# How the expert weights of a two-layer MoE backbone are laid over the partitions when they are loaded

## The chip, the cores and the metric

The kernel runs on one core of one Trainium2 chip. The metric is the device time of one execution in microseconds (us), given as the median of several runs. The kernel before takes 1938.27 us, the median of three runs (1936.55 to 1939.51).

## The reference

The reference is a trunk of two layers over 512 latent tokens and 256 context tokens of width 1024. Layer 0 is attention beside a gated MLP, layer 1 is a bidirectional state-space scan (S5). Each is followed by a mixture of experts, in which every token chooses two of 32 experts, and a last RMSNorm ends it. Cut to what matters here:

```
x = x + m_lat[2] * y_lat                        # mixer of the layer
f = modulate(x, norm_ffn_g, ...)                # (T, 1024); T = 768 in layer 0, 512 in layer 1
top 1 of 4 groups, top 2 of its 8 experts -> two experts and two weights per token
expert e:  (silu(xblk @ w1[e]) * (xblk @ w3[e])) @ w2[e]
           w1[e], w3[e]: (1024, 512)    w2[e]: (512, 1024)    all float32
x = x + m_lat[5] * (sum over a token's two experts of weight * expert(token))
```

The order in which the 1024 features of a token are summed in `xblk @ w1[e]` is free, as long as the features of the tokens and the rows of the matrix are taken in the same order.

## The kernel before

Each layer has a mixer stage and then an expert stage (`moe`, line 1165). In the expert stage `ffn_in` (L884) makes the normalized and modulated features with the features on the partitions (`fT`), multiplies them by the router, and writes the tokens to a DRAM scratch `fD`, one row of 1024 floats per token. For that its inner function `rows` (L918) turns 8 blocks of 128 features by 128 tokens with TensorE into a PSUM tile of 128x1024, copies this to SBUF with ScalarE (L924), and issues the write of 512 KB from ScalarE's queue (L925). There are 6 such tiles in layer 0 and 4 in layer 1. `route` (L944) then makes the tables of which token goes to which expert, on VectorE with small matmuls.

The loop over the 32 experts (L1281) does the following for one expert. GpSimd gathers the expert's tokens from `fD` by an indirect DMA (`gather`, L1088), issued two experts ahead. TensorE turns them (`gathered_T`, L1096) so that the features lie on the partitions in 8 blocks of 128, numbered k. `expert_block` (L1106) then multiplies by W1 and W3, summing over k in PSUM (L1123), forms silu(.) * (.) on ScalarE and VectorE, turns the result (L1135), multiplies by W2 (L1145), weighs it (L1153), and GpSimd scatters it to a DRAM scratch `yD` (L1161). A first block holds 64 tokens; where an expert has more, every engine branches into further blocks (`overflow`, L1254 to L1265). Expert 31 is computed in `finish` (L1328), which also adds both contributions of each token to the residual.

In layer 0 the loop has side work between the experts: `s5_ahead` prepares the S5 parameters of layer 1 on TensorE, VectorE, ScalarE and GpSimd, with small DMAs of its own. One of its results is the DRAM scratch `wD` (L1494), of shape (128, 16, 2, 2, 128). Later, in the mixer of layer 1, `W[i]` is loaded from it in two DMAs (L1859), in each of which partition p takes the block `wD[p, 8*i:8*i+8]`, 8 x 2 x 2 x 128 floats that lie together.

The weights of an expert are three loads of 2048 KB, W1, W3 and W2, issued by SP through `Chunks.load` (L165), `wload` (L211) and `fetch` (L221). `fetch` lets a load start only when the load two before it has landed (`AHEAD = 2`), so that two are in flight. The tiles come from a ring of buffers for some three experts; a load also waits until its buffer was read by the last matmul that used it. Each expert's block ends with `ch.load(3)`, which puts three further loads into SP's order.

The layout of a load is set in L172: `"(k p) n -> p k n"` with p = 128. For W1 and W3, of shape (1024, 512), partition p takes the rows p, 128 + p, ..., 896 + p: 8 rows of 2 KB that lie 256 KB apart. For W2, of shape (512, 1024), it takes 4 rows of 4 KB. Block k of the gathered features meets `Wx[:, k]` in L1123, so feature k * 128 + p of a token meets row k * 128 + p of the matrix.

Of the kernel before, what the change touches and what calls it, by code (L numbers as in the profile page):

```python
# [20 lines left out]
KD = 8  # L21
# [73 lines left out]
class HiLo:  # L95
# [7 lines left out]
    def load(self, m=1):  # L103

        k = self.k
        for _ in range(m):
            r = self.stage.tile([128, self.per, self.n], F32, name="wraw", tag="wraw", bufs=NST2 if self.runs else NST)
            k.fetch(r, self.src[:, self.loaded:self.loaded + self.per])
            self.raw.append(r)
            self.loaded += self.per  # L110
# [48 lines left out]
class Chunks:  # L159
# [5 lines left out]
    def load(self, n=1):  # L165
        k, l = self.k, self.l
        for _ in range(n):
            i = len(self.w)
            if i == 96:
                return  # L170
            e, c = divmod(i, 3)
            src = (k.in_moe_w1, k.in_moe_w3, k.in_moe_w2)[c][l, e].rearrange("(k p) n -> p k n", p=128)  # L172
            pool = self.ring.pop(0)
            self.w.append(k.wload(src, (KD, 512) if c < 2 else (4, 1024), pool=pool))
            if pool is not self.once:
                self.ring.append(pool)


class Kernel:
# [704 lines left out]
    def ffn_in(self, l, tiles, pool, fD, lg):  # L884

        nc = self.nc
        nt = len(tiles)
        t0 = tiles[0]
        wr, br = self.wr, self.br
        A = self.scale1(l, 4, self.gffn[l], f"Affn{l}")  # L890
        S = self.M[l][:, 3]
        fT = pool.tile([128, KD, nt * 128], F32, name="fT")

        spare = [self.X[:, t] for t in range(t0)]
        nf = 5 - t0
        groups = [[(0, NCT, NT - NCT)] + ([(1, 0, NCT)] if t0 == 0 else [])]
        lT = pool.tile([128, 256], F32, name="lT", tag="lT", bufs=1)
        nc.gpsimd.memset(lT, 0.0)
        for tiles_ in self.features(fT, A, S, groups, t0, pool, nf, spare=spare):

            i0, hn = tiles_[0] - t0, len(tiles_) // 2
            q = self.pa([128, hn * 128], name="pl")
            for k in range(KD):
                for h in range(2):
                    at = (i0 + h * hn) * 128
                    nc.tensor.matmul(q[64 * h:64 * h + 36], wr[:, k], fT[:, k, at:at + hn * 128], start=(k == 0),
                                     stop=(k == KD - 1), tile_position=(0, 64 * h))
            for h in range(2):
                hs = slice(64 * h, 64 * h + 36)
                self.evac(lT[hs, :hn * 128], q[hs])  # L910
            p = self.pa([128, hn, 128], name="plT")
            for i in range(hn):
                nc.tensor.transpose(p[:, i], lT[:, i * 128:(i + 1) * 128], self.ident)
            for h in range(2):
                nc.vector.tensor_add(lg[:, i0 + h * hn:i0 + (h + 1) * hn], p[:, :, 64 * h:64 * h + 36],
                                     br[:, None, :].to_broadcast([128, hn, 36]))

        def rows(i):  # L918
            p = self.pb("pfr")
            f = pool.tile([128, D], F32, name="f", tag="fxh", bufs=nf)  # L920
            for k in range(KD):
                self.mark_rows = nc.tensor.transpose(p[:, k // 4, (k % 4) * 128:(k % 4 + 1) * 128],
                                                     fT[:, k, i * 128:(i + 1) * 128], self.ident)
            nc.scalar.copy(f.rearrange("p (a n) -> p a n", a=2), p)  # L924
            nc.scalar.dma_start(fD[i * 128:(i + 1) * 128], f)  # L925

        for i in range(nt):
            rows(i)
# [557 lines left out]
    def s5_ahead(self):  # L1486
# [13 lines left out]
        with ExitStack() as es:  # L1500
# [95 lines left out]
            with tc.tile_pool(name="s5v", bufs=1) as tp:  # L1596
# [43 lines left out]
                def kernel(g2):  # L1640
# [4 lines left out]
                    nc.scalar.copy(kv, p[:, g2 % 2])  # L1645

                load(0)
                yield
                for g2 in range(16):
                    load(g2 + 1)  # L1650
                    s, l = divmod(g2, 2)
                    xs = slice(4 * s + l, 4 * s + 4, 2)
                    br, bi = raw.pop(g2)
                    Q = [x[:, xs, None].to_broadcast([128, 2, 16]) for x in (qr, qi)]
                    b0 = tp.tile([128, 2, 16], F32, name="b0", tag="b0")
                    b1 = tp.tile([128, 2, 16], F32, name="b1", tag="b1")
                    tm = tp.tile([128, 2, 16], F32, name="bt", tag="bt5")
                    self.after(v.tensor_mul(b0, br, Q[0]), self.mark_dve)
                    v.tensor_mul(tm, bi, Q[1])
                    v.tensor_sub(b0, b0, tm)  # L1660
                    v.tensor_mul(b1, br, Q[1])
                    v.tensor_mul(tm, bi, Q[0])
                    v.tensor_add(b1, b1, tm)
                    tm = self.pb("pE")[:, 0, 0:256].rearrange("p (d i q) -> p d i q", d=2, i=8)
                    E[g2] = self.cpair(v, tp, [x[:, xs] for x in le], (b0, b1), 2, "E", 1, tm)
                    yield
                    if g2:
                        kernel(g2 - 1)
                    products(g2)
                    yield  # L1670
# [407 lines left out]
```

## Time and profile before

| what | value |
|---|---|
| median of three runs | 1938.27 us (1936.55 to 1939.51) |
| the profiled execution's own time | 1946.14 us |
| its span (first to last instruction) | 1944.5 us |
| mean granted TensorE clock | 0.918 of full speed |
| read from DRAM, written to DRAM | 513.41 MB, 32.60 MB |
| loads of expert weights | 192 of 2048 KB, on SP's queue |
| expert stage of layer 0, first matmul of expert 0 to that of expert 31 | 450.7 to 1098.5 us |
| expert stage of layer 1, first matmul of expert 0 to that of expert 31 | 1368.6 to 1903.8 us |

All times of the profile belong to one execution, and are counted from the span's start. PE is TensorE, PEld its weight loads, DVE VectorE, ACT ScalarE, POOL GpSimd, SP SyncE; a q behind an engine's name is its sequencer. L1123 is line 1123 of the kernel. Matmuls are pipelined and their ends are modelled, so that TensorE's busy time is no measure of how near it is to its peak. A wait for several semaphores is put down to the one that came last by the profile. Queue q1 holds the DMAs that SP issues, q10 those of ScalarE, q0 GpSimd's; q8 and q14 fetch instructions.

### The profile page before, as it was taken

To read this page: it belongs to the slowest core of one execution; us is meant where nothing else is said; L and a number is where in the kernel's file an instruction comes from. 1 tells how busy PE (TensorE), PEld (TensorE's weight loads), DVE (VectorE), ACT (ScalarE), POOL (GpSimd) and SP (SyncE) were. 2 spreads that over 40 slices of the span, in tenths; PEclk is the share of its full clock that TensorE was granted. 3 is DMA by queue.
4 is the path that set the end of the run, shared out by engine and by line. 5 is a ranking of instruction groups with operands and counts; after the bars stand their busy time and mean duration, and the time that the engine had idled before them with its cause. 6 is when DMAs were issued, how large, how long until landed. Compare 5 with 4: busy or idle time off the path is not lost. (4 is left out here: it accounts for less than half of the span.)

```text
span 1944.5 us, 30168 instructions
## 1 busy us (share of the span) xinstructions
PE 1534.8 (79%) x11383; PEld 976.6 (50%) x11383; DVE 699.3 (36%) x1842; ACT 325.0 (17%) x652; POOL 365.0 (19%) x368
## 2 busy tenths in 40 slices
PE   5999999977777887777678686777888887777765
PEld 3868776654444444444344344455545554344432
DVE  4584544353135323322111299974211110110014
ACT  4323544331000110100000030033100000000002
POOL 1122000112110111111101257552211111111101
PEclk9999999988998998998789888888899998898887
DMA  9331323267999999999869493674899999999993
GB/s 316 119 100 67 131 87 130 87 241 286 361 354 325 351 381 332 384 371 371 293 246 386 174 187 55 218 293 173 306 389 360 385 381 361 363 362 382 378 377 136
DMA packets 268333, 534.73 MB, mean 275 GB/s; under 512 B 48092, under 2 KB 59448, under 8 KB 267696
## 3 DMA queue, kind: packets, MB, share of 16 engines
q1 hardware_dynamic: 224096, 494.96, 70.5%
q0 software_dynamic: 11552, 21.09, 3.1%
q10 hardware_dynamic: 32304, 14.05, 2.8%
q8 instruction: 185, 3.03, 0.7%
q14 instruction: 196, 1.61, 0.2%
HBM read 513.41 MB, written 32.60 MB: 281 GB/s over the span
## 5 line engine op out<-in xcount | busy, mean ns | idle before, releaser
L1123 PE MATMUL ph<-W,xT 128*64 128x256 f32 (+1 forms) x5376 | 577.8, 388 | 190.4 <-DMA W<-in_moe_w_dram 54.4
L1123 PEld LDWEIGHTS ph<-W,xT 128*64 128x64 f32 (+1 forms) x5376 | 397.7, 143 | 382.0 <-issue 188.9
L1145 PE MATMUL py<-W,hT 128*64 128x512 f32 (+1 forms) x1344 | 265.2, 562 | 18.5 <-DMA W<-in_moe_w_dram 6.0
L1129 DVE TENSOR_TENSOR h<-h,ph 128x128 f32<-128x128 f32 x141 | 34.5, 284 | 673.8 <-PE ph L1123 645.5
L1145 PEld LDWEIGHTS py<-W,hT 128*64 128x64 f32 (+1 forms) x1344 | 81.6, 133 | 154.0 <-issue 121.2
L1126 ACT ACTIVATE h<-ph 128x256 f32<-128x256 f32 (+1 forms) x75 | 27.9, 372 | 661.7 <-PE ph L1123 547.0
L1161 POOL DMA_INDIRECT yD<-y,tb0s x62 | 62.7, 1011 | 328.4 <-DVEq L1256 275.8
L1103 ACT COPY xT<-pxT 128x512 f32<-128x512 f32 (+1 forms) x75 | 42.0, 560 | 338.0 <-PE pxT L1101 335.5
L262 PE MATMUL pj<-Whl,hT 128*128 128x512 f32 (+1 forms) x432 | 89.6, 362 | 4.7 <-DVE hT L490 1.2
L1091 POOL DMA_INDIRECT xg<-fD,tb0g x32 | 33.1, 1034 | 301.8 <-PE phT L1135 255.8
L1091 POOL DMA_INDIRECT X<-fD,tb0g x32 | 33.1, 1034 | 265.4 <-PE phT L1135 243.1
L262 PEld LDWEIGHTS pj<-Whl,hT 128*128 128x128 f32 x432 | 70.7, 188 | 19.9 <-DVE hT L490 1.4
L262 PE MATMUL py<-Whl,cat 128*128 128x512 f32 x288 | 70.6, 400 | 0.0
L1153 DVE SCALAR_TENSOR_TENSOR y<-py,tb0w,G 128x512 f32<-128x512 f32 x32 | 24.0, 751 | 115.2 <-PE py L1145 106.1
L262 PEld LDWEIGHTS py<-Whl,cat 128*128 128x128 f32 x288 | 53.4, 188 | 13.7 <-issue 1.4
L1135 PE MATMUL phT<-cpack,h 128*128 128x128 f32 x141 | 41.9, 318 | 21.2 <-DVE h L1129 19.8
L1153 DVE SCALAR_TENSOR_TENSOR y<-py,tb0w,y 128x512 f32<-128x512 f32 x32 | 24.0, 750 | 90.8 <-PE py L1145 90.8
L802 POOL TENSOR_TENSOR X<-X,yg 128x512 f32<-128x512 f32 x12 | 16.5, 1377 | 194.1 <-DVE yg L800 194.1
L741 DVE TENSOR_REDUCE nm<-S 128x1 f32<-128x768 f32 (+1 forms) x48 | 37.1, 775 | 27.2 <-PE S L737 27.2
L375 PE MATMUL pa<-W,sc 128*32 128x512 f32 x288 | 37.8, 646 | 10.6 <-DMA W<-in_w_mod_dram 10.6
L1137 DVE COPY hT<-phT 128x128 f32<-128x128 f32 x141 | 38.9, 291 | 19.6 <-PE phT L1135 19.3
L1876 PE MATMUL pu<-hT,W 128*128 128x384 f32 x128 | 43.8, 502 | 0.0
(515 smaller groups left out, 1958.4 us busy)
## 6 DMA issues: line engine op xcount, KB each, us to landing
W<-in_moe_w_dram SPq DMA_DIRECT2D x192, 2048.0 KB
W<-in_w_mod_dram SPq DMA_DIRECT2D x18, 2048.0 KB
aw<-in_w_mod_dram SPq DMA_DIRECT2D x6, 2048.0 KB
yk<-yD SPq DMA_DIRECT2D x20, 512.0 KB
wraw<-in_mix_w_in_dram SPq DMA_DIRECT2D x14, 512.0 KB
fD<-f ACTq DMA_DIRECT2D x10, 512.0 KB
wD<-w ACTq DMA_DIRECT2D x16, 256.0 KB
W<-wD SPq DMA_DIRECT2D x2, 2048.0 KB
```

What stands on the lines that cost most here:

```text
L262: self.nc.tensor.matmul(p, a[x], b[y], start=start and i == 0, stop=stop and i == 2)
L375: self.after(nc.tensor.matmul(p[32 * j:32 * j + 32], self.sc[:, k], w[:, k], start=(k < 4), stop=(k >= 4), tile_position=(0, 32 * j)), mark)
L741: nc.vector.tensor_reduce(nm, sv, axis=AX.XY, op=OP.max, negate=True)
L1091: self.mark_gather = self.nc.gpsimd.indirect_dma_start(out=xg, out_offset=None, in_=fD.rearrange("t (p n) -> (t p) n", p=parts), in_offset ...
L1103: nc.scalar.copy(xT, p)
L1123: nc.tensor.matmul(ph[w][S * n:S * n + S], lhs, Wx[:, k, n * nh:(n + 1) * nh], start=(k == 0), stop=(k == KD - 1), tile_position=(0, S * n))
L1135: nc.tensor.transpose(p, h[:, q * 128:(q + 1) * 128], self.ident)
L1137: last = nc.vector.tensor_copy(t, p)
L1145: self.mark_pe = nc.tensor.matmul(py[S * n:S * n + S], lhs, W2[:, k, n * ny:(n + 1) * ny], start=(i == 0), stop=(i == 3), tile_position=(0 ...
L1153: self.mark_dve = nc.vector.scalar_tensor_tensor(y, py, wt, gate, op0=OP.mult, op1=OP.mult)
L1161: self.nc.gpsimd.indirect_dma_start(out=yD.rearrange("t (p n) -> (t p) n", p=parts), out_offset=bass.IndirectOffsetOnAxis(ap=si, axis=0), ...
L1876: self.after(nc.tensor.matmul(p, Wi[:, k, 128 * f:128 * f + 128], hT[:, k, 384 * n:384 * n + 384], start=(k == 0), stop=(k == KD - 1)), se ...
```

## The change

W1 and W3 are loaded with `"(p k) n -> p k n"`: partition p takes the 8 neighbouring rows 8 * p to 8 * p + 7, which lie together in DRAM as 16 KB. W2 keeps its layout. Block k of W1 and W3 now holds rows 8 * p + k, so block k of a token's features must hold features 8 * p + k. This is done where the token rows leave PSUM: column k * 128 + q of a row in `fD` now holds feature 8 * q + k. ScalarE's copy reads PSUM with a step of 8 floats for that, and writes the row in order.

```
--- before
+++ after
@@ -169,7 +169,9 @@
             if i == 96:
                 return
             e, c = divmod(i, 3)
-            src = (k.in_moe_w1, k.in_moe_w3, k.in_moe_w2)[c][l, e].rearrange("(k p) n -> p k n", p=128)
+            src = (k.in_moe_w1, k.in_moe_w3, k.in_moe_w2)[c][l, e]
+
+            src = src.rearrange("(p k) n -> p k n" if c < 2 else "(k p) n -> p k n", p=128)
             pool = self.ring.pop(0)
             self.w.append(k.wload(src, (KD, 512) if c < 2 else (4, 1024), pool=pool))
             if pool is not self.once:
@@ -921,7 +923,8 @@
             for k in range(KD):
                 self.mark_rows = nc.tensor.transpose(p[:, k // 4, (k % 4) * 128:(k % 4 + 1) * 128],
                                                      fT[:, k, i * 128:(i + 1) * 128], self.ident)
-            nc.scalar.copy(f.rearrange("p (a n) -> p a n", a=2), p)
+
+            nc.scalar.copy(f.rearrange("p (k q) -> p k q", k=KD), p.rearrange("p a (q k) -> p k (a q)", k=KD))
             nc.scalar.dma_start(fD[i * 128:(i + 1) * 128], f)
 
         for i in range(nt):
```

## Rows read from the trace of the kernel before

**Rows 1.** The page's part 1: busy time, share of the span, instructions.

```profile
PE 1534.8 (79%) x11383; PEld 976.6 (50%) x11383; DVE 699.3 (36%) x1842; ACT 325.0 (17%) x652; POOL 365.0 (19%) x368
```

**Rows 2.** Four stretches: length, busy us (instructions), granted clock, DMA share, GB/s.

```profile
462.00:624.00 162.00, 126.96 (x1079) 73.13 (x1075) 56.68 (x272) 11.85 (x29) 21.34 (x21) 0.94 0.97 354
624.00:904.00 280.00, 222.41 (x1798) 129.35 (x1800) 81.11 (x261) 29.70 (x77) 35.08 (x34) 0.93 1.00 364
904.00:1112.00 208.00, 156.43 (x1324) 88.21 (x1320) 33.53 (x80) 11.17 (x26) 24.97 (x22) 0.88 0.77 280
1372.00:1882.00 510.00, 410.48 (x3109) 239.22 (x3106) 58.15 (x168) 32.74 (x71) 65.75 (x66) 0.94 1.01 374
```

**Rows 3.** SP's waits, 1372 to 1882: us in total, times, longest.

```profile
SPq L222 <- DMA W<-in_moe_w_dram: 447.4, 86, 7.2
```

**Rows 4.** TensorE's waits for weights, 1372 to 1882.

```profile
PE ph L1123 <- DMA W<-in_moe_w_dram: 33.6, 16, 3.5
...
PE py L1145 <- DMA W<-in_moe_w_dram: 4.3, 4, 1.5
```

**Rows 5.** Timeline of TensorE, two neighbouring experts: start, us, work, idle before.

```profile
1539.55 7.13 PE L1123 MATMUL ph<-W,xT 128*64 128x256 f32 x64 [1.43 <-DVEq L1256]
...
1552.69 7.13 PE L1123 MATMUL ph<-W,xT 128*64 128x256 f32 x64 [1.20 <-DVEq L1256]
```

**Rows 6.** DMA queues and issues, 1372 to 1882, last row 624 to 904.

```profile
q8 instruction: 66, 1.08, 0.9%
q14 instruction: 81, 0.66, 0.3%
...
W<-in_moe_w_dram SPq DMA_DIRECT2D x88, 2048.0 KB
...
W<-in_moe_w_dram SPq DMA_DIRECT2D x44, 2048.0 KB
```

**Rows 7.** TensorE's waits, 624 to 904.

```profile
PE ph L1123 <- DMA W<-in_moe_w_dram: 20.9, 7, 4.1
PE ph L1123 <- DVE b L1663: 13.3, 8, 2.3
```

**Rows 8.** SP's waits for weight landings, 462 to 624, then 904 to 1112.

```profile
SPq L222 <- DMA W<-in_moe_w_dram: 93.0, 19, 7.6
...
SPq L222 <- DMA W<-in_moe_w_dram: 88.4, 16, 8.0
```

**Rows 9.** DMA packets in 412:415, 460:463 and 1132:1136; q1: packets, MB, share.

```profile
DMA packets 567, 1.17 MB, mean 388 GB/s; under 512 B 6, under 2 KB 6, under 8 KB 567
q1 hardware_dynamic: 567, 1.17, 104.9%
...
DMA packets 298, 1.22 MB, mean 407 GB/s; under 512 B 0, under 2 KB 0, under 8 KB 298
...
DMA packets 104, 1.70 MB, mean 426 GB/s; under 512 B 0, under 2 KB 0, under 8 KB 0
q1 hardware_dynamic: 104, 1.70, 102.6%
```

**Rows 10.** The page's part 6, the loads from the scratch `wD`.

```profile
W<-wD SPq DMA_DIRECT2D x2, 2048.0 KB
```

**Rows 11.** DMA packets in 1122:1130, the first of these two loads.

```profile
DMA packets 311, 2.40 MB, mean 300 GB/s; under 512 B 31, under 2 KB 31, under 8 KB 183
```

**Rows 12.** Timeline of TensorE from expert 30's W3 to expert 31.

```profile
1876.55 5.20 PE L1123 MATMUL ph<-W,xT 128*64 128x256 f32 x32 [2.38 <-DMA W<-in_moe_w_dram]
...
1898.60 1.94 PE L300 MATMUL pbc<-cpack,fin 128*128 128x128 f32 x8 [12.02 <-PEq L1256]
```

**Rows 13.** Groups on ScalarE by form: busy us, mean ns, idle before.

```profile
L244 ACT COPY PT<-pt 128x384 f32<-128x384 f32 x32 | 15.3, 478 | 40.5 <-PE pt L754 40.3 <-ACT Whl L248 0.2
L924 ACT COPY f<-pfr 128x1024 f32<-128x1024 f32 x10 | 9.7, 1016 | 2.7 <-PE pfr L922 1.7 <-DVE rge L938 0.5 <-DMA fD<-f 0.5
L1879 ACT COPY ut<-pu 128x384 f32<-128x384 f32 x8 | 3.8, 479 | 52.1 <-PE pu L1876 52.1
```

More of the change, by code (lines that the diff above doesn't have):

```diff
@@ L171, in load @@
             e, c = divmod(i, 3)
-            src = (k.in_moe_w1, k.in_moe_w3, k.in_moe_w2)[c][l, e].rearrange("(k p) n -> p k n", p=128)
+            src = (k.in_moe_w1, k.in_moe_w3, k.in_moe_w2)[c][l, e]
+            src = src.rearrange("(p k) n -> p k n" if c < 2 else "(k p) n -> p k n", p=128)
             pool = self.ring.pop(0)
@@ L923, in rows @@
                                                      fT[:, k, i * 128:(i + 1) * 128], self.ident)
-            nc.scalar.copy(f.rearrange("p (a n) -> p a n", a=2), p)
+            nc.scalar.copy(f.rearrange("p (k q) -> p k q", k=KD), p.rearrange("p a (q k) -> p k (a q)", k=KD))
             nc.scalar.dma_start(fD[i * 128:(i + 1) * 128], f)
```

## The prediction

> **What bounds the kernel now.** Start with the page's first line [rows 1]: TensorE is busy for 79% of the span, no other engine above 36%. That average hides stages, so the table of stretches comes next [rows 2]. In the whole of layer 1's expert stage (1372 to 1882 us) and in the middle of layer 0's (624 to 904 us) the 16 DMA engines are 100% busy, while TensorE's modelled busy time leaves about a fifth free. In the first part of layer 0's stage (462 to 624) the share is 97%, in its last part (904 to 1112) 77%.
>
> A busy DMA is a bound only if somebody waits for it. So read the waits of SP, which issues the weight loads two at a time: each load waits until the one two before it has landed. In 1372 to 1882 SP waits 447.4 us, 86 times for 88 loads, for a landing [rows 3]. The load stream hardly stops there, and its own speed sets its end. TensorE's waits say the same from the other side [rows 4]: 33.6 + 4.3 us on weight landings, 20 times. Where weights have landed early, TensorE goes through experts 13.1 us apart (1539.55 to 1552.69, and on) [rows 5]; the loads come 88 in 510 us, three per expert, or 17.4 us per expert [rows 6]. So layer 1 is bound by the loads, with 4 us of TensorE's time to spare on each expert.
>
> In layer 0 the middle stretch is alike: the DMA engines are full [rows 2], and TensorE waits 20.9 us for weights [rows 7]. Outside it the bound is another. In 462 to 624 SP waits for landings 93.0 us of 162, in 904 to 1112 88.4 us of 208 [rows 8]; for the rest of the time it is held up by buffers that TensorE hasn't freed, or busy with other transfers. There, faster loads mostly fill buffers sooner.
>
> **The change part by part.** First, the loads. W1 and W3 of each expert go from 8 separate rows of 512 floats per partition (2 KB each, 1024 pieces per load) to one run of 8 x 512 floats (16 KB, 128 pieces). The bytes, the number of DMA instructions, the tile and the waits stay. W2 keeps its 4 KB rows.
>
> What does the piece size do to the rate? Three stretches of before hold one size each [rows 9]. At 412 to 415 us, 2 KB pieces of W1 and W3: 388 GB/s. At 460 to 463, 4 KB pieces of W2: 407 GB/s. The 16 KB case stands in the trace too: the two loads "W<-wD" of 2048 KB [rows 10] read 16 KB per partition, and at 1132 to 1136 us 104 pieces carry 1.70 MB, none under 8 KB, at 426 GB/s. These have the very form of the changed loads: 128 partitions, 16 KB each, back to back in DRAM. A load of 2.097 MB takes 5.40 us at 388 and 4.92 us at 426, a gain of 0.48 us per load.
>
> The bounds of this price. The better end is hardly above 0.48, as 426 GB/s is a stretch in which every engine is busy. The worse end: over the whole of one such load (1122 to 1130) the mean is 300 GB/s [rows 11], 6.99 us a load, 1.6 us worse than now. That load flew almost alone, so its ragged start and end lie open; in the expert stage the next load fills them. I take 0.48.
>
> The Trainium skill has a rule that speaks against all this: "DMA: Bandwidth & Descriptors", section Specifications, gives 512 B as the smallest transfer for line rate, so that 2 KB would already be enough. By it the gain would be 0, which is rival C below; the rows above disagree, with 388, 407 and 426 GB/s for 2, 4 and 16 KB.
>
> How many loads count? In layer 1 those whose landing TensorE's chain still waits for. The stretch issues 88 loads; two in three are W1 or W3. The last wait on weights is for expert 30, and ends at 1876.55 [rows 12]; the 59 of this kind, less expert 31's two, make 57: 57 x 0.48 = 27.4 us. TensorE can take it, as it has 4 us spare where it needs 1 per expert. In layer 0's middle stretch 44 loads [rows 6] hold 29: 29 x 0.48 = 13.9 us, and TensorE's 20.9 us of weight waits [rows 7] are enough to give that back. The rest of layer 0, 904 to 1112, then runs as it does now, only earlier. Likewise the 12.02 us in which TensorE stands at a branch before the last expert [rows 12], and the tail behind it: they begin when expert 30 is done, and move with it.
>
> Second, the copy. The token rows leave PSUM through ScalarE with a read that steps by 8 floats instead of 1; out are the same 128x1024 floats, 10 times, 1016 ns each now [rows 13]. The same step of 8 stands in line 1879, ut<-pu: 479 ns for 128x384, against 478 ns for the plain copy of that size in line 244 [rows 13]. So 0, and the better end is 0 too, as the element count stays. For the worse end I double the copy, far beyond any row: 10 us, of which TensorE's next transposes, two PSUM buffers behind, would feel most, some 7 us. I take 0.
>
> Nothing else moves: no wait is added, the gather and the transposes see the same shapes, and W1's rows and the token's features are permuted alike.
>
> Sum: 27.4 + 13.9 = 41.3 us. Against the profiled execution (1946.14 us, span 1944.5 and 1.6 around it) that is 1904.8; the median shown is 7.9 lower, and 1938.27 - 41.3 = 1897.0.
>
> **The rivals.** (B) Layer 0 gives nothing. Between its experts TensorE also runs the S5 preparation, and waits 13.3 us on VectorE in that stretch [rows 7]; if such waits take the place of the weight waits, only layer 1 pays: 1938.3 - 27.4 = 1910.9. Against it: the weight waits are the larger, and stand mid-block, between W1 and W3.
>
> (C) No change: the 8 rows stay 8 pieces, or the rate in the mixed stream isn't set by the piece. 1938. For it: the stage averages 374 GB/s, below all three rates. Against it: the wD load, also written as three dimensions (512-byte rows in the program), went out in 16 KB pieces [rows 9].
>
> (D) Slower. A 16 KB piece holds a DMA engine 0.63 us (102.6% of 16 engines x 4 us over 104 pieces), a 2 KB piece 0.09 (104.9% x 16 x 3 over 567) [rows 9]. Instruction fetches run on the same engines: 66 + 81 packets on q8 and q14 in layer 1's 510 us [rows 6], and at that rate some 330 in the 1160 us of all four stretches. If each waits for one large piece and TensorE for each fetch, the price is 330 x 0.54 = 178 us. It wins from 41.3 / 0.54 = 76 exposed fetches on; with 100 the time is 1938.3 + 54 - 41.3 = 1951. For it: TensorE stands 12.02 us at a branch with nothing else named [rows 12]. Against it: most branches cost 1.2 to 1.4 us [rows 5], so most fetches are ahead of their use. Gathers have cover: each is issued two experts ahead. The Trainium skill bears on this case: "DMA: Bandwidth & Descriptors", section Queues, rings and completion order, says that an engine takes turns between queues only at whole packets. No run here shows how a fetch fares beside 16 KB pieces.
>
> (E) More: all 128 loads of W1 and W3 pay, because fuller buffers carry the gain over layer 0's other stretches: 128 x 0.48 = 61.4, 1876.9. Against it: the low DMA share in 904 to 1112 [rows 2].
>
> **How the numbers follow.** Forecast 0.62, B 0.16, C 0.08, D 0.08, E 0.06. The time is the forecast's, 1897. Range 1875 to 1924: from just below E's time to a gain of a third of the forecast's, which takes in B with 13 us to spare for partly exposed fetches or a dearer copy. Left out are C and D, and a little of the rest. A change under 0.2% (about 4 us) can't be told from none here. Faster: forecast, B and E, 0.84; within 0.2%: C, 0.08; slower: D, 0.08.
>
> **What would show it.** Right: in the DMA table most packets of q1 are gone (128 loads x 1024 pieces become 128 x 128); layer 1's load stretch is 25 to 30 us shorter at 390 GB/s or more; SP still waits for landings there; the copy in line 924's place takes about 1016 ns; layer 0's middle stretch is 10 to 15 us shorter. Wrong: the packet count stays (C); TensorE's gaps at branches grow beyond 1.5 us each (D); in layer 0 waits on VectorE or branches replace those on weights (B); the copy takes visibly longer.

## The result, and the profile after

The changed kernel takes 1913.8 us, the median of four runs (1907.4 to 1920.48), against 1938.89 (1936.55 to 1939.77) for the kernel before beside it: a ratio of 0.9873, 95% interval 0.9834 to 0.9911. A second measurement gave 1912.22 (six runs, 0.9857 [0.9815, 0.9899]). So it is faster, by 25 to 27 us where 41 were forecast; rival B's 1910.9 lies nearer than the forecast's 1897.0. The profiled execution is the fastest of the four: 1907.4 us, span 1905.7, mean granted clock 0.929 of full speed.

Part 1 of the page after, which answers to [rows 1], shows nothing of the change but TensorE's shorter busy time:

```profile
PE 1514.8 (79%) x11383; PEld 970.4 (51%) x11383; DVE 697.5 (37%) x1842; ACT 324.7 (17%) x652; POOL 364.4 (19%) x368
```

Part 3 of the page has the pieces. First the kernel before, then after (packets, MB, share of 16 engines):

```profile
q1 hardware_dynamic: 224096, 494.96, 70.5%
```

```profile
q1 hardware_dynamic: 109408, 494.96, 67.9%
```

The difference is 114688 = 128 loads x 896, so every W1 and W3 went from 1024 pieces to 128, at the same bytes.

The four stretches of [rows 2], cut near the same work in the profile after (length, busy us by engine, granted clock, DMA share, GB/s):

```profile
462.00:620.00 158.00, 122.96 (x1070) 71.16 (x1071) 55.65 (x268) 11.84 (x29) 21.35 (x21) 0.95 0.93 362
620.00:895.00 275.00, 225.35 (x1780) 131.70 (x1782) 82.42 (x264) 29.71 (x77) 34.98 (x34) 0.91 0.94 365
895.00:1100.00 205.00, 155.25 (x1342) 86.96 (x1338) 31.81 (x80) 11.17 (x26) 23.86 (x21) 0.90 0.75 284
1360.00:1843.00 483.00, 394.78 (x3112) 235.06 (x3109) 58.34 (x170) 33.21 (x72) 66.30 (x68) 0.98 0.99 394
```

Layer 1's stretch is 27 us shorter (510 to 483) and moves 394 GB/s for 374. The granted clock rose there too, from 0.94 to 0.98, and TensorE was busy for 15.7 us less; no run separates this from the faster loads. Layer 0's middle is only 5 us shorter (280 to 275), and it holds 18 matmuls fewer (1780 for 1798); cut at the same matmul, it is some 2 us shorter. It moves 365 GB/s for 364, and the DMA engines, full before, now stand at 94%. The loads have become faster there and are not issued faster.

SP's and TensorE's waits in layer 1's stretch of the kernel after, which answer to [rows 3, 4] (us, times, longest):

```profile
SPq L224 <- DMA W<-in_moe_w_dram: 403.9, 83, 6.7
SPq L224 <- PEq L1262: 14.6, 3, 7.7
```

```profile
PE ph L1126 <- DMA W<-in_moe_w_dram: 27.5, 17, 2.8
...
PE py L1148 <- DMA W<-in_moe_w_dram: 4.8, 7, 1.5
```

SP still waits for a landing nearly all the time (403.9 us of 483): the stretch is still bound by its loads.

Now layer 0's expert stage as a whole, 462 to 1100 us: what SP waited for before it could issue a weight load, in the kernel before and then after.

```profile
SPq L222 <- DMA W<-in_moe_w_dram: 407.2, 76, 8.9
...
SPq L222 <- DMA rawB<-in_s_b_re_dram: 30.6, 6, 9.1
```

```profile
SPq L224 <- DMA W<-in_moe_w_dram: 317.0, 61, 9.2
SPq L224 <- DMA rawB<-in_s_b_re_dram: 67.6, 9, 11.7
...
SPq L224 <- DMA rawB<-in_s_b_im_dram: 23.1, 5, 7.0
```

The waits for weights fall by 90 us, and 60 come back as waits for `rawB`. These are the parameter transfers of the S5 preparation in `s5_ahead`: 32 DMAs of 16 KB, issued from ScalarE's queue, each of 256 pieces of 64 bytes. No weight load reads them. That SP waits for them is shown here; what ties SP's loads to their landing comes with the experiments.

### The profile page after: what moved, and what is told of

It is laid out like the page before. It is cut to its first block, busy times and chain, and to the rows that moved or that the text cites. A ratio compares the mean times of both kernels' runs of the same rounds, so it can differ in the third digit from the quotient of the medians.

```text
span 1905.7 us, 30168 instructions
## 1 busy us (share of the span) xinstructions
PE 1514.8 (79%) x11383; PEld 970.4 (51%) x11383; DVE 697.5 (37%) x1842; ACT 324.7 (17%) x652; POOL 364.4 (19%) x368
## 3 DMA queue, kind: packets, MB, share of 16 engines
q1 hardware_dynamic: 109408, 494.96, 67.9%
## 5 line engine op out<-in xcount | busy, mean ns | idle before, releaser
L1126 PE MATMUL ph<-W,xT 128*64 128x256 f32 (+1 forms) x5376 | 562.1, 379 | 164.7 <-issue 46.2
L1126 PEld LDWEIGHTS ph<-W,xT 128*64 128x64 f32 (+1 forms) x5376 | 392.3, 139 | 345.8 <-issue 164.1
L264 PE MATMUL py<-Whl,cat 128*128 128x512 f32 x288 | 70.5, 400 | 0.0
```

Source lines behind the costliest of these rows:

```text
L264: self.nc.tensor.matmul(p, a[x], b[y], start=start and i == 0, stop=stop and i == 2)
L1126: nc.tensor.matmul(ph[w][S * n:S * n + S], lhs, Wx[:, k, n * nh:(n + 1) * nh], start=(k == 0), stop=(k == KD - 1), tile_position=(0, S * n))
```

## The experiments

Theory Q: in layer 0 the small transfers on ScalarE's queue fall behind the 16 KB pieces, land late, and hold up SP's next loads and the engines that use them; that eats layer 0's gain, and layer 1, which has no such transfers, pays in full. Rival R: layer 0 paid by the rate as forecast, and the shortfall lies in layer 1. After the first two runs R became: layer 0's stage isn't set by its loads, whatever the small transfers do.

**One layer at a time.** `l0_only` and `l1_only` use the new layout and copy in one layer:

```
-src.rearrange("(p k) n -> p k n" if c < 2 else "(k p) n -> p k n", p=128)
+src.rearrange("(p k) n -> p k n" if c < 2 and l == 0 else "(k p) n -> p k n", p=128)   # l1_only: l == 1
...                            # and the stepped copy under the same condition
```

> Layer 0 alone has the new layout and the stepped copy, layer 1 is as before. Theory Q (queues): the small transfers of the S5 preparation (64-byte pieces of rawB, 2 KB pieces of wD on ScalarE's queue) take turns with 16 KB pieces, land later, and hold up VectorE and SP's next weight loads; layer 0 then keeps little of its 14 us: 1927 to 1941 us, with more scatter from run to run than before. Rival R (rate): layer 0 pays by the rate as forecast, and what is missing in the median is missing in layer 1: 1925 us (14 less), no more scatter. In the profile Q wants SP's waits for rawB at 50 us or more in 624 to 904 us, R about 15.

> Layer 1 alone has the new layout and the stepped copy, layer 0 is as before. Theory Q: layer 1 has no S5 preparation beside its loads and pays in full, 57 x 0.48 = 27 us: 1911 to 1913 us, with as little scatter as before. Rival R: the shortfall of the median (25 measured of 41) lies in layer 1, which gives some 11 us: 1927.

Measured: `l0_only` 1933.91 us, 0.9983 [0.9961, 1.0005]; `l1_only` 1909.66, 0.9861 [0.9836, 0.9886], which is 27 us (1.39% of 1940.09, the kernel before beside it; 30 by the medians). Layer 1 alone is worth as much as the whole change; layer 0 gives nothing that can be told. R's first form is out. SP's waits in `l0_only`, 462 to 1100 us:

```profile
SPq L224 <- DMA W<-in_moe_w_dram: 325.2, 63, 10.3
SPq L224 <- DMA rawB<-in_s_b_re_dram: 72.5, 10, 11.3
...
SPq L224 <- DMA rawB<-in_s_b_im_dram: 17.2, 5, 6.7
```

In `l1_only`, whose layer 0 has 2 KB pieces, the same two waits on `rawB` are 33.5 and 0.5 us.

**The piece size.** `piece8k` and `piece4k` take 4 and 2 neighbouring rows per partition, in both layers, with the copy to match:

```
+src = src.rearrange("(a p j) n -> p a (j n)", p=128, j=4) if c < 2 else src.rearrange("(k p) n -> p k n", p=128)
+w = k.wload(src, (KD // 4, 4 * 512) if c < 2 else (4, 1024), pool=pool)      # piece4k: 2 for 4
...
```

> Both layers; W1 and W3 in 4 neighbouring rows per partition and two blocks (8 KB pieces), the token rows in the matching order. By the rate 8 KB should save about 0.40 us per load (between 0.25 at 4 KB and 0.48 at 16 KB). Theory Q: layer 1 gives 23 us, and layer 0 loses less to taking turns than with 16 KB, so that it keeps 6 to 11: 1905 to 1910, as good as the 16 KB version or better. Rival R: proportionally less than the 16 KB version, 25 x 0.83 = 21 us: 1918.

> Both layers; W1 and W3 in 2 neighbouring rows per partition and four blocks (4 KB pieces, as W2 has them). By the rate 0.25 us per load. Theory Q: layer 1 gives 14 us, layer 0 7 with hardly a loss, as a piece of W2's size was there before: 1918. Rival R: 25 x 0.52 = 13 us: 1926.

Measured: 1914.51 (0.9901 [0.9876, 0.9927]) and 1915.94 (0.9889 [0.9869, 0.9910]). Neither can be told from the changed kernel; Q's hope for 8 KB did not come true. But the waits on `rawB` go by size. `piece8k`, then `piece4k`:

```profile
SPq L225 <- DMA rawB<-in_s_b_re_dram: 60.3, 9, 9.2
SPq L225 <- DMA rawB<-in_s_b_im_dram: 10.2, 4, 4.8
```

```profile
SPq L225 <- DMA rawB<-in_s_b_re_dram: 41.3, 7, 8.6
```

With pieces of 2, 4, 8 and 16 KB SP waits 31.0 (30.6 + 0.4), 41.3, 70.5 and 90.7 us for `rawB`; a second profile of the changed kernel, `after_again`, has 73.5. And layer 1's stage, first matmul of expert 0 to that of expert 31, takes 535.1, 514.0, 511.1 and 507.9 us in the profiles: most of what long pieces give is there at 4 KB. The rates forecast 57 x 0.25 = 14 us for 4 KB, and the stage is 21 shorter. These are single executions: with 2 KB pieces in layer 1 the five profiles run from 528.3 (`l0_only`) to 539.2 (`before_quiet`).

**Without most of the small transfers.** In `after_once`, and in its control `before_once`, 30 of the 32 `rawB` transfers are left out, and all groups use the first group's data:

```
+if g2:
+    raw[g2] = raw[0]
+    return
...
```

> The changed kernel, but only the first of the 16 pairs of small parameter transfers of the S5 preparation (rawB, 256 pieces of 64 bytes each) is made; the 15 later groups use the first group's data, which leaves out 30 of 32 such transfers and makes their values wrong. Theory Q (in layer 0 the small transfers on ScalarE's queue fall behind the 16 KB pieces, and their late landings hold up SP's next weight loads and VectorE, which eats layer 0's gain): SP's and VectorE's waits on rawB, 67.6 + 23.1 + 16.7 us in the profile of the changed kernel, go, SP's waits in layer 0 stand at weight landings again, and layer 0's forecast gain of some 14 us comes out: 0.979 to 0.983 of the kernel before, about 1899 to 1907. Rival R (layer 0's stage is set by TensorE's chain and by buffers, whatever the small transfers do): the waits on rawB turn into waits on weights or buffers, and the time is that of the changed kernel, 0.986 to 0.989.

> The control to the run that makes one pair of rawB transfers only: the same edit on the kernel before, with its 2 KB pieces (30 of 32 rawB transfers left out, values wrong). Theory Q: with 2 KB pieces the small transfers were hardly late (SP waited 30.6 + 0.4 us on them, VectorE 6.1), so little comes of it: 0.995 to 1.000 of the kernel before; the two kernels without these transfers differ by 1.6 to 2% where the two with them differ by 1.3. Rival R: 1.000, and the two without them differ by 1.3% as well.

Measured: 1903.74 (0.9817 [0.9789, 0.9846]) and 1933.45 (0.9970 [0.9949, 0.9990]). The layout is then worth 0.9817 / 0.9970 = 0.9847, 1.5%: between Q's 1.6 to 2% and R's 1.3%, so not decided. The profile of `after_once` (1913.08 us, the slowest of its six runs) named a second transfer, for TensorE (waits, 462 to 640 us):

```profile
PE pC L1528 <- DMA rawC<-in_s_c_im_dram: 6.5, 1, 6.5
```

`rawC` is two sets of 8 DMAs, each of 128 pieces of 256 bytes, also on ScalarE's queue. TensorE's wait for the second set is 6.4 to 7.7 us in four of the six profiles that have 16 KB pieces in layer 0 and `rawC` as it was (`l0_only`, `after_once`, `after_pre`, `after_again`), and absent in all five with 2 to 8 KB pieces there.

**Where the lateness is paid.** `after_pre` issues `rawB` three groups ahead; `after_poolq` issues it from GpSimd's queue at the old place. Nothing is left out.

```
-load(g2 + 1)
+load(g2 + 3)                  # after_pre, with 8 buffers for 4
...
-nc.scalar.dma_start(t, bass.AP(tensor=src.tensor, offset=src.offset + 2048 * g2,
+nc.gpsimd.dma_start(t, bass.AP(tensor=src.tensor, offset=src.offset + 2048 * g2,   # after_poolq
...
```

> The changed kernel, with the rawB transfers issued three groups ahead of their use (8 buffers of 128 bytes per partition for 4), nothing left out. VectorE's waits on rawB (16.7 + 6.1 us) go by either theory. Theory Q: SP still waits for rawB's landings (some 70 to 90 us), as SP's waits on them come from the order of landings and not from VectorE; so a part of layer 0's gain at most, 0.983 to 0.988 of the kernel before. If VectorE's waits were all that ate it: 0.979 to 0.983. Rival R: as the changed kernel, 0.986 to 0.989.

> The changed kernel, with the 32 rawB transfers issued from GpSimd's queue in place of ScalarE's, nothing left out. Theory Q: if SP's waits for rawB come of a completion count that its loads share with ScalarE's transfers, they may go or move to others, while the 64-byte pieces stay beside the 16 KB pieces and land as late, so that VectorE's waits stay: 0.981 to 0.989 of the kernel before. GpSimd's gathers stand behind them in one queue; if these become late, TensorE waits for the gathered tokens and the time rises to 0.990 or more. Rival R: as the changed kernel, 0.986 to 0.989.

Measured: `after_pre` 1918.16 (0.9904 [0.9871, 0.9937]), no better than the changed kernel, though VectorE's waits on `rawB` fell from 16.7 + 6.1 us to 0.6 + 2.1. SP's stayed:

```profile
SPq L224 <- DMA W<-in_moe_w_dram: 341.5, 64, 9.2
SPq L224 <- DMA rawB<-in_s_b_re_dram: 51.0, 7, 10.6
...
SPq L224 <- DMA rawB<-in_s_b_im_dram: 33.1, 3, 18.6
```

`after_poolq` took 1903.92 (0.9813 [0.9784, 0.9842]). In its profile SP has no wait for `rawB` left, and VectorE has 6.4 + 5.3 us of them. So it is SP's weight loads through which `rawB` costs time. SP's first waits in `after_poolq`, 462 to 1100 us:

```profile
SPq L224 <- DMA W<-in_moe_w_dram: 393.9, 75, 8.1
SPq L1342 <- DMA xg<-fD,tb0g: 32.8, 1, 32.8
SPq L224 <- PEq L1259: 32.3, 5, 12.3
SPq L224 <- DMA kkD<-KK: 32.1, 5, 13.2
```

What ties the two stands in the traces too. For each DMA they record the semaphore (a counter) that tells of its landing. The DMAs of SP and of ScalarE share eight of these, numbers 100 and 102 to 108; those of GpSimd have eight others, 111 to 118. Each weight load that SP held up for a landing of `rawB` signals its own landing on the same semaphore as that `rawB` transfer: 7 of 7 in `before`, 14 of 14 in the kernel after, 83 of 83 in the eight profiles that have such waits. So the load waited for the last user of its semaphore, and not for data. From GpSimd's queue `rawB` has other semaphores, and SP's waits for it are gone.

**Both out of the way.** `after_quiet` has `rawB` on GpSimd's queue, and both sets of `rawC` issued together at the start, the second into a buffer of its own. `before_quiet` is the same edit on the kernel before, `l0_quiet` has the new layout in layer 0 alone, `after_again` is the changed kernel unedited.

```
+rawC = []
+for src in (self.in_s5_c_re, self.in_s5_c_im):
+    t = tp.tile([128, 4, 128], F32, name="rawC", tag="rawC", bufs=2)
+    rawC.append(t)
...
+for nm, t, sg in (("Cr", rawC[0], 1.0), ("Cn", rawC[1], -1.0)):
```

> The changed kernel with both kinds of small parameter transfers out of the way: rawB issued from GpSimd's queue, and the second set of rawC (8 transfers of 128 pieces of 256 bytes, for which TensorE waited 6.4 to 7.7 us in three of the five profiles with 16 KB pieces in layer 0 and rawC on this schedule) issued early, with the first set, into a buffer of its own. Nothing is left out. Theory Q (small transfers that fall behind 16 KB pieces eat layer 0's gain): TensorE's wait for rawC is gone in the profile, SP has no waits for rawB, and some 4 us more come out than with rawB alone on GpSimd's queue (0.9813): 0.976 to 0.981 of the kernel before, 1893 to 1903, with less scatter from run to run. Rival R (layer 0's stage isn't bound by its loads, and what moves it is chance): 0.981 to 0.988.

> The control: the same two moves on the kernel before. Theory Q: with 2 KB pieces neither transfer was late (no wait of TensorE for rawC, SP's waits for rawB 30.6 us), so 0.995 to 1.000 of the kernel before; the layout is then worth 1.8 to 2.2% between the two kernels with the moves (forecast 41.3 us, 2.1%), against 1.3% between the two without. Rival S (the moves help either kernel alike and have nothing to do with the piece size): 0.992 to 0.995, and the layout is worth 1.3% with them as without.

> The new layout in layer 0 alone, with the two moves of small transfers. Without the moves it gave 0.9983 of the kernel before, nothing that can be told. Theory Q: layer 0's forecast 13.9 us now come out in good part, 0.989 to 0.994 of the kernel before, and 8 to 14 us below the kernel before with the moves. Rival R: layer 0 gives nothing even so, the same time as the kernel before with the moves within 4 us.

> The changed kernel itself once more, unedited, beside the three with the moved transfers on the same chip, so that they can be compared directly. Either theory: 0.985 to 0.990 of the kernel before, 1909 to 1920. In the profile TensorE's wait for the second rawC set is there (6 to 8 us) if the run's profile is above 1910, and absent if it is near 1906, by theory Q; by rival R there is no such link.

| kernel | layout in layer 0 / 1 | small transfers | median (runs) | ratio to before |
|---|---|---|---|---|
| before | 2 KB / 2 KB | as they were | 1938.71 (22) | 1 |
| `after_again` | 16 / 16 | as they were | 1912.22 (6) | 0.9857 [0.9815, 0.9899] |
| `before_quiet` | 2 / 2 | moved | 1934.56 (12) | 0.9991 [0.9961, 1.0021] |
| `l0_quiet` | 16 / 2 | moved | 1922.46 (11) | 0.9919 [0.9889, 0.9950] |
| `after_quiet` | 16 / 16 | moved | 1895.88 (6) | 0.9788 [0.9750, 0.9826] |

Moving the small transfers alone gives nothing that can be told (0.9991; 4 us by the medians). With them moved, the layout is worth 0.9991 - 0.9919 = 0.72% in layer 0 (14.0 us) and another 1.31% in layer 1 (25.4 us): 39.4 us in all, where 13.9 + 27.4 = 41.3 were forecast. The medians give 12.1, 26.6 and 38.7. Taking the intervals as independent, layer 0's 14.0 is known to within 8 us and the sum to within 10. By the times R falls, and so does S, by which the moves would help either kernel alike.

The profiles, of one execution each, don't confirm this at the place. Layer 0's stage, first matmul of expert 0 to that of expert 31, takes 647.8 us in `before`, 633.3 in `before_quiet`, 629.1 in `l0_quiet` and 626.8 in `after_quiet`; the changed kernel has 637.1 and, in `after_again`, 645.1. By these the moves alone shorten the stage by 14.5 us, as S would have it, and the layout then adds 4.2 to 6.5. Two profiles of one kernel lie 8 us apart, so this decides nothing, but how much of layer 0's gain needs both changes together rests on the times alone.

`after_quiet` is the best version, and its six runs lie within 8 us (1892.32 to 1900.05), those of `after_again` within 13. Its SP waits, 462 to 1100 us, and then TensorE's instructions on `rawC`, whose only idle time is now that at a branch:

```profile
SPq L224 <- DMA W<-in_moe_w_dram: 400.8, 76, 8.4
SPq L224 <- PEq L1259: 40.3, 8, 10.8
SPq L224 <- DMA kkD<-KK: 32.5, 5, 13.7
```

```profile
544.03 0.66 PE L1531 MATMUL pC<-cpack,rawC 128*128 128x128 f32 x4
...
558.92 0.63 PE L1531 MATMUL pC<-cpack,rawC 128*128 128x128 f32 x4 [1.10 <-DVEq L1259]
```

The run `after_again` had its profile at 1912.54 us, and the wait for `rawC` in it as Q expects there:

```profile
556.19 0.55 PE L1528 MATMUL pC<-cpack,rawC 128*128 128x128 f32 x3 [1.20 <-DVEq L1259]
563.38 0.45 PE L1528 MATMUL pC<-cpack,rawC 128*128 128x128 f32 x1 [6.65 <-DMA rawC<-in_s_c_im_dram]
```

How the lateness arises can in part be read from the DMA packets between the issue of the set's last DMA and the set's last landing. The kernel before, 545.9 to 552.4 us (packets, MB, share):

```profile
q1 hardware_dynamic: 862, 1.77, 80.9%
...
q10 hardware_dynamic: 314, 0.08, 5.5%
```

And `after_again`, 543.8 to 562.3 us:

```profile
DMA packets 1398, 7.48 MB, mean 404 GB/s; under 512 B 526, under 2 KB 526, under 8 KB 1086
...
q1 hardware_dynamic: 868, 7.14, 95.1%
...
q10 hardware_dynamic: 405, 0.10, 2.7%
```

Before, 314 small pieces of q10 passed in 6.5 us, after, 405 in 18.5. The two windows are not alike: before, the weight stream used only 45.1% of the engines in the first 2.1 us, and 178 of the 314 passed there. Two parts with a full weight stream compare better, 550 to 552.4 us before and 554 to 562.3 in `after_again`:

```profile
q1 hardware_dynamic: 434, 0.89, 98.5%
q10 hardware_dynamic: 136, 0.03, 6.3%
```

```profile
q1 hardware_dynamic: 218, 3.19, 91.8%
...
q10 hardware_dynamic: 60, 0.01, 0.8%
```

There 3.2 and 3.6 weight pieces went by for each small one, while the weight pieces had grown from 2.05 KB to 14.6 KB on average. So the small queue gets its turns by pieces rather than by bytes, as far as two windows can tell; the turns aren't even, as from 548 to 550 us before no small piece passed beside 340 weight pieces. The Trainium skill says in "DMA: Bandwidth & Descriptors", section Queues, rings and completion order, that an engine changes to another queue only between whole packets, and it counts several descriptors to a packet. The trace agrees in that turns don't go by bytes; how many of the profile's pieces make one such turn no run shows.

## Why the prediction was right in part

**The price per load: right at 16 KB.** 4 us of layer 1's stretch in which W1 and W3 alone fly, 1376 to 1380 in the profile after, show

```profile
DMA packets 122, 1.74 MB, mean 434 GB/s; under 512 B 16, under 2 KB 16, under 8 KB 16
...
q1 hardware_dynamic: 121, 1.72, 101.4%
```

434 GB/s, where 426 were taken from the `wD` load [rows 9]; the ragged 300 GB/s [rows 11] did not come. Rival C is out: layer 1 gained 1.39% from the layout and the copy that goes with it. By the same number this case disagrees with the 512 B that the prediction took from the Trainium skill, "DMA: Bandwidth & Descriptors", section Specifications.

Two readings behind the price were weaker than they look. The `wD` pieces do not have "the very form of the changed loads": with the shape (128, 16, 2, 2, 128) their starts lie 32 KB apart, and are not back to back in DRAM. That made no difference that can be seen (426 and 434 GB/s). And the series of rates did not price 4 KB, where 14 us were forecast and layer 1's stage became 21 shorter.

**Layer 1, 27.4 us: right.** Its stage takes 507.9 us in the profile for 535.1, that is 27.2 less, and `l1_only` gains 27 us. The 57 loads by 0.48 us and the claim that TensorE has the time to follow hold. That the two agree to 0.2 us is luck: profiles with the same layout in layer 1 lie up to 11 us apart. TensorE's 12.02 us at the branch [rows 12] came along, as said:

```profile
1859.88 1.94 PE L302 MATMUL pbc<-cpack,fin 128*128 128x128 f32 x8 [11.91 <-PEq L1259]
```

**Layer 0's middle stretch, 13.9 us: the step that failed.** "TensorE's 20.9 us of weight waits are enough to give that back" looked only at whether TensorE could use faster loads, and "Nothing else moves: no wait is added" left out what else flew beside them. The waits that were added are SP's for `rawB` (31.0 us before, 90.7 and 73.5 after) and TensorE's 6.65 for `rawC` in `after_again`. Alone, this term measured 3 us (`l0_only`, 0.17%, interval -1 to 8). In the profile after, TensorE's weight waits in layer 0 do fall, from 22.6 us to 9.4 over 462 to 1100; in that of `after_again` they are 20.7 again. With the small transfers out of the way the term came to 12 to 14 us by the times, known to within 8, and to 4 to 6 by the profiles: its size may have been right, or lucky.

The sign of it stood in the trace of before. What SP waits in 462 to 624 us beside the landings of weights, the prediction put down to buffers and other transfers. It is 53.9 us, and 37.7 of them are waits for landings of ScalarE's small transfers:

```profile
SPq L222 <- DMA rawB<-in_s_b_re_dram: 15.9, 2, 9.1
SPq L222 <- DMA rawC<-in_s_c_re_dram: 11.1, 1, 11.1
SPq L222 <- PEq L1256: 10.9, 3, 4.3
SPq L222 <- DMA rawC<-in_s_c_im_dram: 10.7, 1, 10.7
```

**The copy, 0: right.** It answers to [rows 13] with 1015 ns for 1016:

```profile
L927 ACT COPY f<-pfr 128x1024 f32<-128x1024 f32 x10 | 9.7, 1015 | 2.7 <-PE pfr L924 1.7 <-DVE rge L941 0.5 <-DMA fD<-f 0.5
```

**Rival B had the time and not the reason.** Its VectorE waits did not take the place of the weight waits: in layer 0's middle TensorE waits 18.2 us on VectorE's S5 work after, for 17.3 before. Its other sign, waits at branches, shows in part: those on ScalarE's sequencer there went from 8.5 us to 13.4. **Rival D had the reason and not the place.** A long piece does make small packets of other queues wait, but TensorE's waits at branches, over the two expert stages, are 70.5 us after for 67.9 before; instruction fetches, D's case, hardly suffered. The small transfers that did were ScalarE's data, whose count on q10 (9357 packets in 624 to 904) stands in the same view as the 35 and 46 of q8 and q14. The prediction priced the fetches and did not ask who waits for these.

**What stays open.** Why the second `rawC` set is late in four profiles of six and in time in two, and how much of layer 0's gain the moves would have brought without long pieces (nothing that can be told by the times, 14.5 us by one profile). How the 16 to 18 us between the changed kernel and `after_quiet` divide is known roughly: about 9 with `rawB` moved (1903.9 for 1912 to 1914), about 8 more with `rawC`, of which TensorE's direct wait is 6.6.

## What to carry to other kernels

Longer pieces speed up a stream that somebody waits for, and can make small-piece transfers that share the engines with it late. Before lengthening them, list the other queues' transfers in the same stretch by pieces (a 16 KB parameter load is 256 pieces of 64 bytes), look for who waits for their landing, loads that share a semaphore with them included, and move those out of the way first: here that raised the gain from 26 us to 43 by the medians. If they can't be moved, lengthen the pieces only in the stage that has none: layer 1 alone gave all that the whole change gave.

## What the runs showed of the hardware

Four rates of a full DMA stream into 128 partitions were seen: 388 GB/s at 2 KB, 407 at 4 KB, 426 and 434 at 16 KB. A ScalarE copy that reads PSUM with a step of 8 floats takes as long as a plain one (1015 and 1016 ns for 128x1024). And the semaphore of a transfer decides whose waits its lateness reaches: in this program SP's and ScalarE's DMAs share eight, and `rawB` from ScalarE held up SP's loads for 90.7 us (73.5 in a second profile); GpSimd's have eight others, and `rawB` from GpSimd, at the same place and with the same pieces, held up none.
